# The opening of an encoder layer: x loaded in two halves with the first w_ada group between, and a tile pair of four column pairs by plain blocks

## The chip, the cores and the metric

One core of one Trainium2 chip runs the whole layer in one launch. The metric is the device time of one execution in microseconds (us). TensorE (PE) does the matmuls, VectorE (DVE) and ScalarE (ACT) the element-wise work, GpSimd (POOL) a few small things, and SyncE (SP) issues nearly all DMAs, in the order in which they were written to its queue.

## The reference

Everything is float32. x is (1024, 2048), D = 2048; c is one vector. Cut to what matters here:

```python
mod = silu(c) @ w_ada + b_ada                 # w_ada: (2048, 6144)
shift, scale, gate = split(mod, 3)
h = rmsnorm(x, pre_g) * (1 + scale) + shift   # (1024, 2048)
q, k, v, gate_a, u, gate_p = split(h @ w_in)  # w_in: (2048, 4608)
y_a = windowed_gqa(q, k, v, rel_table, sink) * silu(gate_a)
y_p = multiscale_pool(u, w_pool_grp, pool_scale) * silu(gate_p)
g_a, g_p = split(sigmoid(h @ w_merge + b_merge))   # w_merge: (2048, 4096)
merged = g_a * (y_a @ w_br_attn) + g_p * (y_p @ w_br_pool)
out = x + gate * rmsnorm(merged @ w_out, post_g)
```

The change concerns the way into `h @ w_in`: how x, w_ada and the first columns of w_in come in, and in which order the first products are made.

## The kernel before, in words

**Precision and Strassen.** A float32 operand is kept as two float32r halves, high and low (`split`: ACT copies the high half, DVE subtracts it to get the low one), and a product takes three matmuls: high by high, high by low, low by high. A product of 256 output columns by 1024 rows of x over a part of D is done as one level of Strassen's scheme (`strassen`): seven products X, V, Z, X, V, Z, Z with the moving operands B11, T3, T2, B21, T4, T1, B22. These are made from the four quarters of a pair of tiles of h transposed (two tiles of 128 columns of D, each in a left half of 512 rows of x, s = 0, and a right half, s = 1). A *pair* is such a block of 256 columns of the combined w_in and w_merge: 34 pairs in all. `js` lists the tile pairs of D that a call covers; the first half of D has tile pairs 0 to 3. A pair with two tile pairs has 7 x 3 x 2 = 42 matmuls of 128x512, with four 84.

**The ramp.** At the start h isn't there yet. It becomes ready one tile pair after the other, so the first RAMP = 5 pairs are done in two parts: first over tile pairs 0 and 1, results put away in `ramp_d`, then over tile pairs 2 and 3, with the first part added. The very first pair takes its tile pairs 0 and 1 by *plain blocks* instead (four blocks of 128x512, six matmuls each per tile pair, no Strassen sums). The other pairs of the first pass (`pass1`) take all four tile pairs at once.

**How h comes about.** `fetch_rows_of_x` loads eight groups of 128 rows, four tiles of 512 columns each (256 KB a load). `norm_rows` squares and sums them (two tiles on ACT, two on DVE), takes root and reciprocal, and makes `turn`: a diagonal matrix of 1/rms. `turn_rows` and `turn_round` multiply x's tiles by it on TensorE, which transposes and scales in one go (two matmul records each). `modulation(j)` makes scale and shift for tile pair j: a GEMV over 16 tiles of w_ada (four steps q of eight records), a copy to SBUF (`acc`), four transposes into PM, and DVE's sums into `modc`. `fill(j)` modulates tile pair j and makes all seven moving operands, each high and low; `fill_blocks` and `fill_sums` are the same work in two halves, for the plain blocks and for Strassen.

**Order.** The program is traced and then laid out by a scheduler that goes by priority in program order and by free buffers; instructions handed to `keep` stay in the written order on their engine. The opening is written out by hand in this way. In the ramp, `side` holds steps that are taken one at each of the seven places of a pair (the groups of w_ada for tile pairs 2 and 3, `late_sums`); in the first pass `side` holds the sums of w_ada for the second half of D, taken at the places in `EASY`.

**Buffers that matter.** 56 tiles of 2 KB a partition (`big`) for x, w_ada's groups, xT and the moving operands; four for raw weights; nine `ev` tiles for results on their way out; PSUM tags `mm`, `sc`, `at` with two banks each and `z0`, `z1` (SEEDED) with one.

Of the kernel before, what the change touches and what calls it, by code (L numbers as in the profile page):

```python
# [13 lines left out]
F32 = mybir.dt.float32  # L14
# [29 lines left out]
def encoder_layer(ctx: ExitStack, tc: tile.TileContext, x, c, table, w_ada, b_ada, pre_g,  # L44
# [89 lines left out]
    RAMP = 5  # L134
# [55 lines left out]
    def load_raws(w, n0, rows, js, pin=False):  # L190

        raws = []
        nj = len(js)
        joint = wp.tile([P, 2, nj, 256], F32, tag="raw", name=uid("raw"), bufs=4) if nj < 4 else None
        for kh in range(2):
            r = joint[:, kh] if nj < 4 else wp.tile([P, nj, 256], F32, tag="raw", name=uid("raw"), bufs=4)
# [216 lines left out]
    def norm_rows(si):  # L413
        ssq = ep.tile([P, 8], F32, tag="ssq", name=f"ssq{si}", bufs=4)
        for q in range(4):
            xt = xts[si, q]
            if q < 2:
                junk = bank("sc", "junk")
                ins = nc.scalar.activation(junk, xt, AF.Square, accum_out=ssq[:, q:q + 1])
                if si < 2:  # L420
                    keep(ins)
            else:
                junk = bank("at", "junk")
                nc.vector.scalar_tensor_tensor(junk, xt, 1.0, xt, op0=ALU.mult, op1=ALU.mult,
                                               accum_out=ssq[:, q:q + 1])
        nc.vector.tensor_reduce(ssq[:, 4:5], ssq[:, 0:4], op=ALU.add, axis=AX.X)
        if si == 0:
            small_vectors()
        ins = nc.scalar.activation(ssq[:, 5:6], ssq[:, 4:5], AF.Sqrt, bias=eps_t, scale=1.0 / D)
        if si < 2:  # L430
            keep(ins)
        nc.vector.reciprocal(rstd[:, si:si + 1], ssq[:, 5:6])
# [3 lines left out]
        nc.vector.tensor_scalar(turn[si], ident, rstd[:, si:si + 1], None, op0=ALU.mult)  # L436

    def turn_round(s, q, js):

        banks = [bank(t, "XT1") for t in SEEDED]  # L440

        def turn_one(m, n):
            keep(nc.tensor.matmul(banks[n][:, m * P:(m + 1) * P], xts[4 * s + m, q][:, js[n] * P:(js[n] + 1) * P],
                                  turn[4 * s + m], start=True, stop=True))

        def put_by(both=False):
            if both:
                keep(nc.scalar.activation(xT[q * 4 + js[0], s], banks[0], AF.Copy))
            else:
                keep(nc.vector.tensor_copy(xT[q * 4 + js[0], s], banks[0]))  # L450
            keep(nc.scalar.activation(xT[q * 4 + js[1], s], banks[1], AF.Copy))

        return deque(partial(turn_one, m, n) for m in range(4) for n in range(2)), put_by

    def turn_rows(s):

        for q in range(1):
            banks = [bank(t, "XT1") for t in ("mm", "mm", *SEEDED)]
            for m in range(4):
                for j in range(4):  # L460
                    nc.tensor.matmul(banks[j][:, m * P:(m + 1) * P], xts[4 * s + m, q][:, j * P:(j + 1) * P],
                                     turn[4 * s + m], start=True, stop=True)
            for j in range(4):
                if j % 2 == 0:
                    nc.vector.tensor_copy(xT[q * 4 + j, s], banks[j])
                else:
                    nc.scalar.activation(xT[q * 4 + j, s], banks[j], AF.Copy)
# [132 lines left out]
    def fill_blocks(j, between=None):  # L600

        (b11, b12), (b21, b22) = ((xT[k, 0], xT[k, 1]) for k in (2 * j, 2 * j + 1))
        right = tuple(bp.tile([P, 512], F32R, tag=t, name=uid(t)) for t in ("B12h", "B12l"))
        for n, ((hi, lo), t, k) in enumerate(((op["B11"][j], b11, 2 * j), (op["B21"][j], b21, 2 * j + 1),
                                              (right, b12, 2 * j), (op["B22"][j], b22, 2 * j + 1))):
            keep(modulate(nc.scalar, t, k, hi))
            keep(modulate(nc.vector, t, k))
            if n < 3 or between:
                anchor["blocks"] = sub(lo, t, f32(hi))
                keep(anchor["blocks"])  # L610
            if between:
                between(n)
        return right

    def fill_sums(j, done=False):
# [6 lines left out]
        if not done:  # L622
            hi, lo = op["B22"][j]
            keep(sub(lo, b22, f32(hi)))
# [6 lines left out]
    def ramp_gen(jj, i, parts, **kw):  # L631
        w, n0 = weight_of(ORDER[i])
        dst = block(part_d, ORDER[i]) if jj else block(ramp_d[i], 0)
        return strassen(w, n0, rows_in_turn(0), (2 * jj, 2 * jj + 1), op, ev, to_dram(dst), parts, raws[i], **kw)

    fetch_rows_of_x(0)
    fetch_rows_of_x(1)
    raws = []

    def fetch_raws(i):  # L640
        raws.append(load_raws(*weight_of(ORDER[i]), rows_in_turn(0), [0, 1], True))

    def fetch_half(j):
        w, n0 = weight_of(ORDER[0])
        for kh in range(2):
            keep(load(raws[0][kh][:, j], rows_in_turn(0)(w, [0, 1], kh)[:, j, n0:n0 + 256]))

    ada = [ada_slots(0)]
    joint = wp.tile([P, 2, 2, 256], F32, tag="raw", name=uid("raw"), bufs=4)
    raws.append([joint[:, 0], joint[:, 1]])  # L650
    fetch_half(0)
    ada.append(ada_slots(1))
    fetch_half(1)
    fetch_raws(1)
    fetch_raws(2)
    claim(0)
    ada.append(ada_slots(2))
    claim(1)
    fetch_raws(3)
    ada3 = [ada_tile(3, q) for q in range(5)]  # L660
    ada3 = [at[:, kk] for at in ada3 for kk in range(2)] + ada_slots(3, range(10, KT))
    for i in range(4, RAMP):
        fetch_raws(i)
# [3 lines left out]
    late_sums = {0: group2[:1], 4: group2[1:4], 5: group2[4:], 10: group3[:4], 12: group3[4:]}  # L667
    side = deque((lambda n=n: [step() for step in late_sums.get(n, ())]) for n in range(13))
    for s in range(2):
        for si in range(4 * s, 4 * s + 4):  # L670
            norm_rows(si)
        if s == 0:
            bias_rows()
        turn_rows(s)
    keep(nc.vector.tensor_scalar(nsink_t, sink_t, -1.0, None, op0=ALU.mult))
    weights0 = []

    def first_weights(j):
        hi, lo = (wp.tile([P, 2, 256], F32R, tag=t, name=uid(t), bufs=4) for t in ("whi", "wlo"))
        for kh in range(2):  # L680
            split(hi[:, kh], lo[:, kh], raws[0][kh][:, j], True)
        weights0.append((hi, lo))

    opened, right_top = {}, []

    def plain_block(blk, j):

        nt, s = int(blk[0]) - 1, int(blk[1]) - 1

        def piece(n):  # L690
            if j == n == 0:
                opened[blk] = bank("mm" if s == 0 else "sc", "PB")
            whi, wlo = (w[:, :, nt * P:(nt + 1) * P] for w in weights0[j])
            mov = (op["B11"][j], op["B21"][j]) if s == 0 else (right_top[j], op["B22"][j])
            kh, w, m = ((0, whi, 0), (0, wlo, 0), (1, whi, 0), (1, wlo, 0), (0, whi, 1), (1, whi, 1))[n]
# [991 lines left out]
```

## Time and profile before

| what | value |
|---|---|
| median of 3 runs | 2103.34 us (2102.85 to 2106.11) |
| profiled execution: its span, first to last instruction | 2099.7 us; its own time is told by this span alone, 3.6 us under the median of the runs |
| TensorE busy | 2073.3 us, 99% |
| DVE, ACT busy | 1540.1 us (73%), 1108.6 us (53%) |
| mean granted TensorE clock | 0.998 |
| moved by DMA | 468.20 MB, 223 GB/s over the span |
| first 46.4 us: TensorE busy | 29.22 us, DMA share 0.97 |

How to read the rows that follow. A row of the timeline has the start in us, the duration, engine, source line, operation, what it writes <- what it reads, shape and count, and in brackets how long the engine had been idle before it and what ended that. "PEld" are weight loads, which run beside the matmuls. A busy TensorE isn't TensorE at its peak: ends of matmuls are modelled, so rates are read from starts. A DMA row on SPq is the time of issue; the list of DMA issues gives the median time from there to landing.

### The profile page before, as it was taken

The page shows a single profiled execution, that of the slowest core. Times are in us where ns is not written, and L with a number is a line of the kernel's source. Part 1 is how long each engine was busy: PE and PEld are TensorE (multiplying, and loading weights), DVE is VectorE, ACT ScalarE, POOL GpSimd, SP SyncE. Part 2 cuts the span into 40 slices and gives each one's busy share as a digit, 9 for nine tenths or more (in the row PEclk, how much of TensorE's full clock was granted, in tenths as well). Part 3 has the DMA queues.
Part 4 walks back from the last instruction along what each step waited for, and adds up shares of the span by engine and source line. Part 5 has one row for each costly group of instructions (what it writes and reads, how often), then busy time and mean ns, then how long its engine had stood idle before and what let it go on. Part 6 is the DMA issues. An engine that isn't in the chain of part 4 may idle for free.

```text
span 2099.7 us, 28891 instructions
## 1 busy us (share of the span) xinstructions
PE 2073.3 (99%) x9511; PEld 1709.1 (81%) x9511; DVE 1540.1 (73%) x2769; ACT 1108.6 (53%) x2105; POOL 33.9 (2%) x119
## 2 busy tenths in 40 slices
PE   6999999999999999999999999999999999999998
PEld 4688888888888888888888888888888888888886
DVE  5886777777556766677777678857857977889667
ACT  4754444444574635665665444333645644767654
POOL 0000000000000000000000000010000000000000
PEclk9999999999999999999999999999999999999999
DMA  9888788887675455454554476675745566686997
GB/s 328 292 273 270 226 270 284 273 280 243 214 241 193 136 187 189 158 174 159 186 164 155 160 246 214 217 243 178 251 159 175 168 201 197 225 308 206 292 339 246
DMA packets 302251, 468.20 MB, mean 223 GB/s; under 512 B 23939, under 2 KB 144875, under 8 KB 302100
## 3 DMA queue, kind: packets, MB, share of 16 engines
q1 hardware_dynamic: 297024, 453.60, 66.0%
q0 software_dynamic: 3616, 10.53, 1.3%
q10 hardware_dynamic: 1460, 2.22, 0.3%
q8 instruction: 74, 1.21, 0.2%
q14 instruction: 77, 0.63, 0.1%
HBM read 341.45 MB, written 126.90 MB: 223 GB/s over the span
## 4 chain that ended last, share of the span: by engine, by line
PE 94%; DVE 1%; DMA 1%; ACT 0%; issue 0%; DVEq 0%; SPq 0%; ACTq 0%
PE Z L247 32%; PE X L247 21%; PE V L247 21%; PE Z L1394 2%; PE Z L1396 2%; PE Z L1395 2%; PE X L1396 1%; PE V L1396 1%; PE V L1394 1%; PE X L1394 1%; PE X L1395 1%; PE V L1395 1%; PE PT L1104 1%; PE PV L1115 0%; PE PV L1116 0%; PE PV L1114 0%
## 5 line engine op out<-in xcount | busy, mean ns | idle before, releaser
L96 ACT ACTIVATE whi<-raw 128x512 fp32r<-128x512 f32 (+1 forms) x532 | 321.7, 606 | 517.9 <-PE Z L247 250.9
L97 DVE TENSOR_TENSOR wlo<-raw,whi 128x512 fp32r<-128x512 f32 (+1 forms) x532 | 347.4, 658 | 168.1 <-PE Z L247 133.1
L97 DVE TENSOR_TENSOR wlo<-wr,whi 128x512 fp32r<-128x512 f32 x224 | 150.6, 689 | 50.7 <-ACT whi L96 43.4
L96 ACT ACTIVATE whi<-wr 128x512 fp32r<-128x512 f32 x224 | 138.5, 629 | 86.6 <-DVE wlo L97 29.4
L114 DVE TENSOR_TENSOR raw<-raw,raw 128x512 f32<-128x512 f32 x79 | 54.6, 691 | 85.1 <-DMA raw<-in_w_merge_dram 61.9
L96 ACT ACTIVATE whi<-ws 128x512 fp32r<-128x512 f32 (+1 forms) x88 | 53.7, 610 | 71.6 <-PE X L247 63.8
L247 PE MATMUL Z<-T1h,whi 128*128 128x512 f32 x334 | 91.0, 390 | 0.0
L247 PE MATMUL Z<-B22h,whi 128*128 128x512 f32 x334 | 90.9, 392 | 0.0
L247 PE MATMUL X<-B21h,whi 128*128 128x512 f32 x334 | 90.9, 391 | 0.0
L247 PE MATMUL X<-B11h,whi 128*128 128x512 f32 x334 | 90.7, 390 | 0.0
L247 PE MATMUL V<-T3h,whi 128*128 128x512 f32 x334 | 90.7, 391 | 0.0
L247 PE MATMUL V<-T4h,whi 128*128 128x512 f32 x334 | 90.5, 391 | 0.0
L247 PE MATMUL Z<-T2h,wlo 128*128 128x512 f32 x334 | 90.2, 390 | 0.2 <-DVE wlo L97 0.2
L247 PE MATMUL X<-B11l,whi 128*128 128x512 f32 x334 | 90.4, 390 | 0.0
L247 PE MATMUL Z<-T2h,whi 128*128 128x512 f32 x334 | 90.2, 390 | 0.2 <-ACT whi L96 0.2
L247 PE MATMUL Z<-T1l,whi 128*128 128x512 f32 x334 | 90.3, 389 | 0.0
L247 PE MATMUL Z<-B22l,whi 128*128 128x512 f32 x334 | 90.2, 390 | 0.0
L247 PE MATMUL X<-B21l,whi 128*128 128x512 f32 x334 | 90.2, 390 | 0.0
L247 PE MATMUL V<-T3l,whi 128*128 128x512 f32 x334 | 90.2, 390 | 0.0
L247 PE MATMUL V<-T4l,whi 128*128 128x512 f32 x334 | 90.2, 389 | 0.0
L247 PE MATMUL Z<-T1h,wlo 128*128 128x512 f32 x334 | 90.1, 389 | 0.0
L247 PE MATMUL V<-T3h,wlo 128*128 128x512 f32 x334 | 90.1, 389 | 0.0
(364 smaller groups left out, 4822.0 us busy)
## 6 DMA issues: line engine op xcount, KB each, us to landing
part<-part_d SPq DMA_DIRECT2D x136, 256.0 KB, 4.7
ada<-in_w_ada_dram SPq DMA_DIRECT2D x128, 256.0 KB, 5.8
raw<-in_w_merge_dram SPq DMA_DIRECT2D x64, 512.0 KB, 5.4
raw<-in_w_in_dram SPq DMA_DIRECT2D x62, 512.0 KB, 4.0
wr<-ws_dS SPq DMA_DIRECT2D x60, 512.0 KB, 5.3
wr<-in_w_out_dram SPq DMA_DIRECT2D x48, 512.0 KB, 5.2
proj_d<-part SPq DMA_DIRECT2D x68, 256.0 KB, 2.2
sw<-in_w_out_dram SPq DMA_DIRECT2D x64, 256.0 KB, 5.5
```

Source lines behind the costliest of these rows:

```text
L96: ins = (nc.scalar.activation(hi, src, AF.Copy), nc.vector.tensor_tensor(lo, src, f32(hi), ALU.subtract))
L97: nc.vector.tensor_tensor(lo, src, f32(hi), ALU.subtract))
L114: return (eng or nc.vector).tensor_tensor(o, a, b, ALU.add)
L247: nc.tensor.matmul(ps, w_[:, i], op[mov][j][m_], start=fresh and i == 0 and n == 0, stop=i == nj - 1 and n == 2, skip_group_check=True)
L1104: nc.tensor.transpose(pt[:, i * P:(i + 1) * P], p[:, i * P:(i + 1) * P], ident)
L1394: nc.tensor.matmul(pb, hi, w[0], start=first, stop=False, skip_group_check=True)
L1395: nc.tensor.matmul(pb, lo, w[0], start=False, stop=False, skip_group_check=True)
L1396: nc.tensor.matmul(pb, hi, w[1], start=False, stop=last, skip_group_check=True)
```

## The change

- The loads' order on SP: rows 0 to 511 of x, w_ada's first group, 512 columns of w_in for tile pair 0 (`wide`, four loads), then rows 512 to 1023, w_ada's second group, and the weights of the next pairs.
- Four pairs (K, V, and the first two of gate_a) take tile pair 0 by plain blocks, 16 blocks of six matmuls; their second part then covers tile pairs 1, 2 and 3. Four more pairs take tile pairs 0 and 1 by Strassen and then 2 and 3. RAMP is 8.
- The left half (s = 0) of all eight tiles of x's first half of columns is turned at once. Then the eight left blocks are written in turn with `norm_rows` 4 to 7 (all kept now, with the squares written over x's own tiles of columns 1024 to 2047), with `turn_first` (the first two tiles of the right half) and with `scale_rows`, which scales the other six tiles on ACT so that `turn_later` can turn them by a plain transpose.
- `fill_half` replaces `fill_blocks`. Tile pair 1 has no plain blocks: its GEMV comes between the last right blocks, and `fill(1)` is unpinned ahead of the ramp.
- The groups of w_ada for tile pairs 2 and 3 are summed at steps 13 to 25 of the ramp, not 0 to 12. The first pass has 17 pairs in its first stretch, not 20, with up to five side steps a pair.

```diff
-    RAMP = 5
+    AHEAD_PAIRS = 4
+    RAMP = 8
...
-        joint = wp.tile([P, 2, nj, 256], F32, tag="raw", name=uid("raw"), bufs=4) if nj < 4 else None
+        joint = wp.tile([P, 2, nj, 256], F32, tag="raw", name=uid("raw"), bufs=4) if nj < 3 else None
...
     def norm_rows(si):
-        for q in range(4):
-            xt = xts[si, q]
-            if q < 2:
-                junk = bank("sc", "junk")
...
+        for q in (2, 3, 0, 1):
+            xt, junk = xts[si, q], xts[si, q | 2]
+            if q % 2 == 0:
+                keep(nc.scalar.activation(junk, xt, AF.Square, accum_out=ssq[:, q:q + 1]))
             else:
+                keep(nc.vector.scalar_tensor_tensor(junk, xt, 1.0, xt, op0=ALU.mult, op1=ALU.mult,
+                                                    accum_out=ssq[:, q:q + 1]))
...
     def turn_rows(s):
-        for q in range(1):
+        for q in range(2):
...
+    def turn_first(m):
+        for k in range(2):
+            if m == 0:
+                late_banks[k] = bank(SEEDED[k], "XT1")
+            keep(nc.tensor.matmul(late_banks[k][:, m * P:(m + 1) * P], xts[4 + m, 0][:, k * P:(k + 1) * P],
+                                  turn[4 + m], start=True, stop=True))
+
+    def scale_rows(si):
+        for q, c0 in ((0, 2 * P), (1, 0)):
+            part = xts[si, q][:, c0:512]
+            keep(nc.scalar.activation(part, part, AF.Copy, scale=rstd[:, si:si + 1]))
+
+    def turn_later(k, n):
+        pt = bank(SEEDED[n % 2], "XT2")
+        for m in range(4):
+            keep(nc.tensor.transpose(pt[:, m * P:(m + 1) * P], xts[4 + m, k // 4][:, k % 4 * P:(k % 4 + 1) * P], ident))
+        if n % 2:
+            keep(nc.vector.tensor_copy(xT[k, 1], pt))
+        else:
+            keep(nc.scalar.activation(xT[k, 1], pt, AF.Copy))
...
+    def fill_half(s):
+        names = ("B11", "B21") if s == 0 else ("B12", "B22")
+        for k, name in enumerate(names):
+            src = xT[k, 0] if s == 0 else late_banks[k]
...
+            keep(modulate(nc.scalar, src, k, hi))
+            keep(nc.vector.tensor_scalar(xT[k, s], src, modc[:, 1, k, 0:1], modc[:, 0, k, 0:1],
+                                         op0=ALU.mult, op1=ALU.add))
+            keep(sub(lo, xT[k, s], f32(hi)))
...
     fetch_rows_of_x(0)
+    ada = [ada_slots(0)]
+    fetch_wide(0)
+    fetch_wide(1)
+    claim(0)
     fetch_rows_of_x(1)
     ada.append(ada_slots(1))
+    ramp_raws(4, (0, 1))
+    ramp_raws(5, (0, 1))
+    claim(1)
     ada.append(ada_slots(2))
+    ramp_raws(6, (0, 1))
     ada3 = [ada_tile(3, q) for q in range(5)]
...
+    ramp_raws(7, (0, 1))
...
-    late_sums = {0: group2[:1], 4: group2[1:4], 5: group2[4:], 10: group3[:4], 12: group3[4:]}
+    late_sums = {13: group2[:1], 16: group2[1:4], 17: group2[4:], 23: group3[:4], 25: group3[4:]}
...
+    def plain_block(i, nt, s):
+        ps = bank(("mm", "sc")[blocks[0] % 2], "PB")
+        whi, wlo = (w[:, :, nt * P:(nt + 1) * P] for w in weights0[i])
+        mov = (op["B11"][0], op["B21"][0]) if s == 0 else (right["B12"], op["B22"][0])
+        for n, (kh, w, m) in enumerate(((0, whi, 0), (0, wlo, 0), (1, whi, 0), (1, wlo, 0), (0, whi, 1), (1, whi, 1))):
+            keep(nc.tensor.matmul(ps, w[:, kh], mov[kh][m], start=n == 0, stop=n == 5, skip_group_check=True))
+        t = ev.tile([P, 512], F32, tag="ev", name=uid("c"))
+        if blocks[0] % 2:
+            keep(nc.vector.tensor_copy(t, ps))
+        else:
+            keep(nc.scalar.activation(t, ps, AF.Copy))
+        store(block(ramp_d[i], 0)(f"{nt + 1}{s + 1}"), t)
+        blocks[0] += 1
+
+    g0 = modulation(0, ada[0].__getitem__, True)
+    for step in g0[:4]:
+        step()
+    wide_weights(0)
+    fill_half(0)
+    wide_weights(1)
+    norm_rows(4)
+    plain_block(0, 0, 0)
+    plain_block(0, 1, 0)
+    turn_first(0)
+    scale_rows(4)
+    wide_weights(2)
+    plain_block(1, 0, 0)
+    norm_rows(5)
+    plain_block(1, 1, 0)
+    turn_first(1)
+    scale_rows(5)
...
+    plain_block(3, 0, 0)
+    norm_rows(7)
+    plain_block(3, 1, 0)
+    turn_first(3)
+    fill_half(1)
+    scale_rows(7)
...
+    plain_block(0, 0, 1)
+    turn_next(1)
+    plain_block(0, 1, 1)
+    turn_next(1)
+    fill_sums(0)
+    plain_block(1, 0, 1)
+    turn_next(2)
+    plain_block(1, 1, 1)
+    turn_next(2)
+    s0, s1, s2, s3, _ = modulation(1, ada[1].__getitem__, True)
+    plain_block(2, 0, 1)
     s0()
+    plain_block(2, 1, 1)
     s1()
+    plain_block(3, 0, 1)
     s2()
+    s3()
+    plain_block(3, 1, 1)
...
     held.close()
+    fill(1)
...
-    EASY = ((0, 2, 4, 6), (1, 3, 5))
-    n1 = 20
+    EASY = ((0, 2, 4, 6), (0, 1, 3, 5, 6), (0, 2, 4, 6))
+    n1 = PAIRS - RAMP - 9
```

More of the change, by code (lines that the diff above doesn't have):

```diff
@@ L435, in norm_rows @@
         turn[si] = turn["all"][:, (si % 4) * P:(si % 4 + 1) * P]
[L436 to L453, printed above, removed]
+        keep(nc.vector.tensor_scalar(turn[si], ident, rstd[:, si:si + 1], None, op0=ALU.mult))
     def turn_rows(s):
-        for q in range(1):
+        for q in range(2):
             banks = [bank(t, "XT1") for t in ("mm", "mm", *SEEDED)]
@@ L636, in encoder_layer @@
     fetch_rows_of_x(0)
+    ada = [ada_slots(0)]
+    fetch_wide(0)
+    fetch_wide(1)
+    claim(0)
     fetch_rows_of_x(1)
[L638 to L649, printed above, removed]
@@ L684, in encoder_layer @@
[L684 to L695, printed above, removed]
-            keep(nc.tensor.matmul(opened[blk], w[:, kh], mov[kh][m], start=j == n == 0,
-                                  stop=j == 1 and n == 5, skip_group_check=True))
-            if j == 1 and n == 5:
-                t = ev.tile([P, 512], F32, tag="ev", name=uid("c"))
-                keep(nc.scalar.activation(t, opened[blk], AF.Copy))
-                store(block(ramp_d[0], 0)(blk), t)
-        return [partial(piece, n) for n in range(6)]
```

175 lines of the change are left out of this document (59 added, 116 removed).

## The prediction

> **What bounds the kernel now.** I read the page first (busy shares, the chain that ended last), then busy time by stage, then the first 113 us instruction by instruction.
>
> ```profile
> span 2099.7 us, 28891 instructions
> PE 2073.3 (99%) x9511; PEld 1709.1 (81%) x9511; DVE 1540.1 (73%) x2769; ACT 1108.6 (53%) x2105; POOL 33.9 (2%) x119
> PE 94%; DVE 1%; DMA 1%; ACT 0%; issue 0%; DVEq 0%; SPq 0%; ACTq 0%
> 0.00:46.40 46.40, 29.22 (x151) 20.51 (x152) 21.20 (x71) 22.64 (x58) 3.02 (x34) 0.93 0.97 326
> 46.40:69.50 23.10, 22.53 (x117) 13.05 (x117) 20.69 (x42) 14.01 (x26) 1.24 (x14) 1.00 1.09 346
> 69.50:112.50 43.00, 43.00 (x224) 31.32 (x221) 38.53 (x88) 32.89 (x73) 0.00 (x0) 1.00 0.83 270
> 160.00:540.00 380.00, 380.00 (x1685) 312.63 (x1684) 271.59 (x402) 159.65 (x260) 6.73 (x13) 1.00 0.80 263
> 183.68 5.44 PE Z L247 x24
> ```
>
> (Stage rows: length, then busy time and count of PE, weight loads, DVE, ACT, POOL, then granted clock, DMA share, GB/s.) TensorE works without a gap from 69.5 us on and carries 94% of the chain; 24 of its 128x512 matmuls take 5.44 us, 0.227 each. So only two things can move the time: how many matmuls are left when TensorE becomes dense, and any new gap behind that point. Ahead of 46.4 us it waits for loads; from 46.4 to 69.5 it stood still 0.6 us in all. The reference point is the first V product behind the opening:
>
> ```profile
> 69.48 0.73 PE L247 MATMUL V<-T3h,whi 128*128 128x512 f32 x2
> ```
>
> **The change, by parts.** The loads are the first part.
>
> ```profile
> 0.74 11.40 SPq L411 DMA_DIRECT2D xt<-in_x_dram  x15
> 11.71 8.03 SPq L411 DMA_DIRECT2D xt<-in_x_dram  x12
> 24.09 5.87 SPq L497 DMA_DIRECT2D ada<-in_w_ada_dram  x9
> xt<-in_x_dram SPq DMA_DIRECT2D x48, 256.0 KB, 5.4
> ada<-in_w_ada_dram SPq DMA_DIRECT2D x128, 256.0 KB, 5.8
> 42.19 0.14 PEld L512 LDWEIGHTS GEMV<-ada,scz 128*32 128x32 f32 x2 [0.61 <-DMA ada<-in_w_ada_dram]
> ```
>
> The fifteenth load of x has been issued by 12.1 us; the sixteenth follows and lands 5.4 later, near 18. A load of x takes 0.67 us of the queue (12 in 8.03), one of w_ada 0.75 (256 KB at 346 GB/s). With 16 loads of x ahead of w_ada's first group, not 32, that group has landed at 18 + 16 x 0.75 = 30, not 42.2; the four `wide` loads at 33; rows 4 to 7 of x at 35.7, 38.4, 41.1 and 43.7; w_ada's second group at 55.7.
>
> From the last landing to the first plain block I take the rows of before, 12.2 us earlier:
>
> ```profile
> 43.27 0.60 ACT L519 ACTIVATE acc<-GEMV 128x512 f32<-128x512 f32 x1 [1.75 <-PE GEMV L512]
> 45.53 0.81 ACT L567 ACTIVATE B11h<-xT,modc 128x512 fp32r<-128x512 f32 x1 [1.06 <-issue]
> 46.40 0.50 PE L696 MATMUL PB<-B11h,whi 128*128 128x512 f32 x1 [0.71 <-ACT B11h L567]
> 48.28 0.69 DVE L117 TENSOR_TENSOR B21l<-xT,B21h 128x512 fp32r<-128x512 f32 x1
> 49.02 0.50 PE L696 MATMUL PB<-B21l,whi 128*128 128x512 f32 x1
> ```
>
> So acc at 31.1, first block at 34.2, its last half (B21l) at 36.8. This is the gain: plain blocks start 12.2 us sooner.
>
> What follows loses it. Eight blocks of the left half stand in one written order with rows 4 to 7, and every instruction of that order is kept. On ACT the copy of a block (`plain_block` i,0,0) stands ahead of the next row's squares (`norm_rows`). The rows of one such round:
>
> ```profile
> 13.22 0.58 ACT L419 ACTIVATE junk<-xt 128x512 f32<-128x512 f32 x1
> 13.83 0.58 ACT L419 ACTIVATE junk<-xt 128x512 f32<-128x512 f32 x1
> 27.71 0.16 DVE L426 TENSOR_REDUCE ssq<-ssq 128x1 f32<-128x4 f32 x1
> 28.42 0.29 DVE L436 TENSOR_SCALAR turn<-ident,rstd 128x128 f32<-128x128 f32 x1
> 28.76 0.38 PE L461 MATMUL XT<-turn,xt 128*128 128x128 f32 x1 [0.41 <-DVE turn L436]
> 64.59 1.09 ACT L700 ACTIVATE c<-PB 128x512 f32<-128x512 f32 x2
> 35.86 2.05 PE L443 MATMUL XT<-turn,xt 128*128 128x128 f32 x16
> ```
>
> Two tiles turned (4 records of 0.12 each): 0.5. A block, 6 x 0.227: 1.4, and 0.2 to its end. Its copy 0.55. Two squares at 0.61, with their read 1.4. Reduce to the next turning (27.71 to 28.76) 1.05. Together 5.1 us a row, of which TensorE has 3.3 us of work: 1.8 us lost in each round. The first turning comes at 40.05 (DVE: 36.8, two weight splits to 37.4, two squares to 39.0, then 1.05); the others at 45.2, 50.3, 55.4. The right half's first block then starts at 56.8 (B12h 0.8 us) and ends at 59.2 with its low half. Rows have landed by 43.7, so loads don't set this.
>
> Next, two blocks, two turned tiles, and `fill_sums(0)`:
>
> ```profile
> 51.13 0.68 DVE L117 TENSOR_TENSOR xT<-xT,xT 128x512 f32<-128x512 f32 x1
> 57.16 0.69 DVE L97 TENSOR_TENSOR T1l<-xT,T1h 128x512 fp32r<-128x512 f32 x1
> 55.46 1.06 PE L512 MATMUL GEMV<-ada,scz 128*32 128x512 f32 x8
> 43.94 0.64 PE L480 MATMUL PM<-ident,acc 128*128 128x128 f32 x4
> ```
>
> Those sums took 6.7 us, 6.1 without the B22l that moves. They start at 62.7 (behind two DVE copies) and end at 68.8. The copies that free banks z0 and z1 for the fifth and sixth turned tile stand behind them on ACT and DVE, so TensorE stands still from 65.4 to 69.2 and has its last tile at 70.3. Then four blocks (1.36 each) and four steps of GEMV (1.05 each, 8 records) with the last block behind them: GEMV done at 78.5, though its data landed at 55.7. `modc` is ready 2.3 later (43.27 to 45.53) at 80.8. `fill(1)` must make T3 low before V's fourth matmul: two scalings, three sums in a chain (51.13 and its like), five more of 0.6 each on DVE, 6.3 us, so 87.1. V then counts as started at 86.4.
>
> Matmuls: four pairs by 24 plain and 63 Strassen (7 x 3 x 3), 87 against 84; before, one pair by 48 + 42. That is +6. At V after, 48 more plain ones are behind it: 42 fewer left, -9.5 us; and 8 GEMV records more, +1.1. The 24 turned tiles in one record each (0.16 in PM's row, against 0.26 in XT's) lie ahead of V. Opening: 86.4 - 69.5 - 9.5 + 1.1 = **+8.5 us**.
>
> Later group sums: the third GEMV's columns come at step 25 of 28, so `fill(3)` has two Strassen products before the second half begins.
>
> ```profile
> 91.79 0.60 PE L480 MATMUL PM<-ident,acc 128*128 128x128 f32 x4
> 94.54 0.16 DVE L490 SCALAR_TENSOR_TENSOR modc<-modc,cols 128x2 f32<-128x2 f32 x1
> 104.20 0.69 DVE L97 TENSOR_TENSOR T3l<-xT,T3h 128x512 fp32r<-128x512 f32 x1
> 112.70 0.61 PE L247 MATMUL X<-B11h,whi 128*128 128x512 f32 x2
> ```
>
> Here T3l came 13.1 us after PM on a DVE that was full (38.53 of 43.0), and nobody waited. After, V of the second half wants it 0.6 + 2 x 1.36 + 9 x 0.227 + 5 x 0.227 = 6.5 us after PM. Upper bound 13.1 - 6.5 = 6.6; lower, on an idle DVE (43.94 to 45.53 is 1.6, then 6.3, less 6.5), 1.4. I take **+4.0**, between them, since pairs 6 and 7 leave DVE some room.
>
> Queues. SP takes the loads in the new order without a stop up to w_ada's second group: of the 56 `big` buffers 12 hold xT, 16 x's first half, 16 w_ada's first group, and the later ones come free by 31 us. The third group does wait: 12 + 14 + 14 + 16 buffers are full until the second GEMV runs, so it is issued from about 72 on and lands by 72 + 16 x 0.75 + 5.8, near 91; step 13 asks for it at 86.4 + 12 x 1.36 = 103. POOL's 14 marks of `claim(1)` wait for x's second half (70.3) and are wanted at 80.8. Both cost nothing; if step 13 came at 86, the same wait would be 5 us.
>
> At nothing too: `scale_rows` (8 ACT copies, 4 us; ACT waits for blocks meanwhile; in the open at most 1 us for the last row); squares written to SBUF (0.1 us a square either way); three more pairs in two parts (6 MB more, at the 0.83 and 0.80 DMA share of the stages above there is room; cover gone, 6 MB at 346 GB/s is 18 us of queue, some 3 us of wait); 4.3 side steps a pair, not 3.5, in the first pass (DVE busy 72%, TensorE 19 us a pair). Ends 0 and +3 for the last two.
>
> Sum: 2103.3 + 8.5 + 4.0 = 2116 us, made against the span of 2099.7, which lies 3.6 under the median of the runs shown.
>
> A word on the clock.
>
> ```profile
> 21.30:24.70 3.40, 0.65 (x7) 0.49 (x5) 3.19 (x10) 3.02 (x9) 0.00 (x0) 1.00 1.06 395
> 24.70:28.10 3.40, 3.40 (x16) 3.40 (x16) 2.63 (x10) 2.01 (x9) 0.00 (x0) 0.50 1.05 382
> ```
>
> A stretch of 3.4 us with TensorE busy for 0.65 was followed by one at half clock. The gap of 3.8 us at 65.4 could do the same: 3.4 us at half, +1.7, so 2118. I leave it out, since stretches that straddle the gap are busy in part. The Trainium skill (TensorE: Matmul & The Clock Gate, HAM oscillation — how this bites in real kernels) asks for no idle gap over about 3.4 us; by that rule the sum would be 2118, and these two rows agree with it.
>
> **Rivals.**
> Faster: TensorE stays dense from the first plain block, as it did from 46.4 to 69.5. Work from 34.2 to V: 104 matmuls 23.6, turned tiles 5.8, GEMV 4.2: 67.8; from the last GEMV step to T3 low are 8.6 us, and one block, X and half of V cover 3.9 of them: 72.5. Opening 72.5 - 69.5 - 9.5 + 1.1 = -5.4; with the low 1.4 for `fill(3)`: 2099. It needs each row's scale ready while blocks run, a round of 3.3 us. Against it: two ACT squares and the copy are kept in order.
> No change: the squares overlap the block ahead of them (three rounds, -5.4), `fill_sums(0)` doesn't queue behind the two DVE copies (-1.4), and `fill(3)` costs its low end: 2103.3 + 8.5 - 6.8 + 1.4 = 2106. The remaining gap behind `fill_sums` and the late GEMV eat the earlier start. For it speaks that DVE and ACT have idle time in every round; against it, as above, the written order.
> Slower still: the copies' buffers.
>
> ```profile
> 80.27 2.58 SPq L701 DMA_DIRECT2D ramp_d<-c  x4
> ramp_d<-c SPq DMA_DIRECT2D x12, 256.0 KB, 5.2
> 86.04 0.60 ACT L320 ACTIVATE c<-Z 128x512 f32<-128x512 f32 x1 [1.68 <-DMA ramp_d<-c]
> ```
>
> Copies ready at 66 were stored at 80.3, behind loads, and ACT waited for a buffer. After, 16 copies go through the same nine; the tenth is wanted at 61.5. If 14 loads (two pairs' weights and ten of w_ada's, 10.5 us) stand ahead of the first store on SP, which is through with w_ada's second group and two pairs at 53, that store lands at 53 + 10.5 + 5.2 = 69: +7.5, 2123. It decides as soon as the first store is issued after 56. Against it: the first three copies are ready by 43, ahead of those loads.
>
> **How the numbers follow.** The forecast (2109 to 2122 alone) 0.56, buffers 0.14, no change 0.13, faster 0.17. Faster or slower means by over 0.2%, 4.2 us, about what a measurement tells apart: slower 0.70, same 0.13, faster 0.17. The range 2098 to 2125 reaches from the faster rival to the buffers with 2 us.
>
> **What would show it.** First plain block near 34; turnings of x's second half about 5 us apart with TensorE idle between; a gap of about 4 us behind `fill_sums(0)`; the second GEMV near 72 to 78; V near 86; a wait for T3l when the second half begins. Wrong if the rounds are near 3.3 us, if row loads land after 50, or if TensorE is dense before 75.

## The result, and the profile after

The changed kernel takes 2132.8 us (median, 2130.3 to 2135.6), the kernel before 2103.6: a ratio of 1.0139 (95% interval 1.0124 to 1.0153), 29.2 us slower. The forecast was +12.7 (2116, range 2098 to 2125): right in sign, too small by 16.5 us.

The page, then busy time by stage (length, busy time and count of PE, weight loads, DVE, ACT and POOL, granted clock, DMA share, GB/s):

```profile
span 2133.8 us, 28930 instructions
PE 2079.5 (97%) x9493; PEld 1709.6 (80%) x9493; DVE 1554.5 (73%) x2790; ACT 1111.6 (52%) x2111; POOL 33.3 (2%) x119
PE 92%; DMA 4%; DVE 3%; ACT 1%; issue 0%; SPq 0%; DVEq 0%; POOL 0%; ACTq 0%; POOLq 0%
```

```profile
0.00:35.89 35.89, 18.81 (x104) 13.11 (x104) 12.43 (x41) 15.72 (x36) 2.33 (x34) 0.90 0.94 307
35.89:59.80 23.91, 17.49 (x65) 12.35 (x65) 14.73 (x43) 15.36 (x39) 0.59 (x6) 0.86 1.06 353
59.80:93.90 34.10, 24.97 (x120) 15.20 (x120) 20.65 (x39) 14.87 (x28) 0.79 (x8) 0.95 0.66 223
93.90:139.60 45.70, 44.27 (x226) 30.67 (x224) 30.88 (x70) 29.66 (x60) 0.00 (x0) 1.00 0.62 211
139.60:163.20 23.60, 15.40 (x56) 12.45 (x57) 18.10 (x34) 10.45 (x20) 0.00 (x0) 0.78 0.67 215
```

Before, TensorE was dense from 46.4 us on but for 0.6 us. Here it stands still for 6.4 us in the left half (second row), for 9.1 in the right half and the fill (third), and for 8.2 once more at 140 us (fifth), a place that had no gap before. The chain of work tells the same: TensorE's share fell from 94% to 92%, DMA's rose from 1% to 4%.

To see where the 29 us come in, I compared the times at which equal numbers of Strassen matmuls are left in both traces: +17.0 at 139 us, just ahead of the last stand, +28.3 at 163 us, about +31 at 410, +34 at the end. (Between 94 and 139 us the count doesn't compare, since the two kernels sum w_ada's later groups at different places.) Of the 17.0, 1.4 are a wait at 108.6 us, so some 15.6 belong to the opening. The profiled execution is 2.8 us above its median and that of the kernel before some 2 us below its own, so the traces show about 5 us more than the medians. What TensorE waited for from 34 to 165 us (total, times, longest):

```profile
PE X L248 <- ACT whi L96: 8.2, 1, 8.2
PE XT L467 <- ACT xT L471: 5.4, 1, 5.4
PE XT L454 <- DVE turn L431: 5.2, 3, 1.7
PE PB L697 <- ACT B11h L571: 1.6, 1, 1.6
```

The timeline at the two largest waits (in brackets the idle time of the engine and what ended it):

```profile
55.80 21.15 SPq L703 DMA_DIRECT2D ramp_d<-c  x12
65.26 0.42 ACT L96 ACTIVATE whi<-raw 128x256 fp32r<-128x256 f32 x1 [0.75 <-PE PB L697]
65.70 0.42 DVE L97 TENSOR_TENSOR wlo<-raw,whi 128x256 fp32r<-128x256 f32 x1 [2.54 <-ACT whi L96]
68.04 0.68 DVE L117 TENSOR_TENSOR xT<-xT,xT 128x512 f32<-128x512 f32 x1
70.28 0.42 ACT L96 ACTIVATE whi<-ws 128x256 fp32r<-128x256 f32 x1 [4.60 <-PE PB L697]
74.72 0.68 DVE L97 TENSOR_TENSOR T1l<-xT,T1h 128x512 fp32r<-128x512 f32 x1
75.62 1.97 PE L467 MATMUL XT<-ident,xt 128*128 128x128 f32 x8 [5.38 <-ACT xT L471]
88.34 0.16 DVE L494 SCALAR_TENSOR_TENSOR modc<-modc,cols 128x2 f32<-128x2 f32 x1
...
141.34 1.57 SPq L198 DMA_DIRECT2D raw<-in_w_in_dram  x3
147.22 0.52 ACT L96 ACTIVATE whi<-raw 128x384 fp32r<-128x384 f32 x1 [2.09 <-DMA raw<-in_w_in_dram]
147.80 1.65 PE L248 MATMUL X<-B11h,whi 128*128 128x512 f32 x3 [8.21 <-ACT whi L96]
```

`fill_sums(0)` ran from 68.04 to 75.4 (forecast: 62.7 to 68.8). Among and ahead of its kept instructions stand weight splits of the fifth ramp pair (`whi`, `wlo`, `ws`), which are not kept and were put there by the scheduler. They wait for buffers that plain blocks still read. The second half's first weights went out at 141.34, right behind the last pair's stores on SP.

### The profile page after: what moved, and what is told of

The parts are those of the page before. It is cut to its first block, busy times and chain, and to the rows that moved or that the text cites. A ratio compares the mean times of both kernels' runs of the same rounds, so it can differ in the third digit from the quotient of the medians.

```text
span 2133.8 us, 28930 instructions
## 1 busy us (share of the span) xinstructions
PE 2079.5 (97%) x9493; PEld 1709.6 (80%) x9493; DVE 1554.5 (73%) x2790; ACT 1111.6 (52%) x2111; POOL 33.3 (2%) x119
## 4 chain that ended last, share of the span: by engine, by line
PE 92%; DMA 4%; DVE 3%; ACT 1%; issue 0%; SPq 0%; DVEq 0%; POOL 0%; ACTq 0%; POOLq 0%
PE Z L248 30%; PE X L248 20%; PE V L248 20%; PE Z L1388 2%; PE Z L1390 2%; PE Z L1389 2%; PE X L1389 1%; PE X L1390 1%; PE X L1388 1%; PE V L1389 1%; PE V L1388 1%; PE V L1390 1%; PE PT L1098 1%; DMA ada<-in_w_ada_dram 1%; PE PB L697 1%; DMA xt<-in_x_dram 1%
## 5 line engine op out<-in xcount | busy, mean ns | idle before, releaser
L96 ACT ACTIVATE whi<-raw 128x512 fp32r<-128x512 f32 (+2 forms) x528 | 319.3, 606 | 529.7 <-PE Z L248 261.3
L97 DVE TENSOR_TENSOR wlo<-raw,whi 128x512 fp32r<-128x512 f32 (+2 forms) x528 | 344.2, 655 | 172.1 <-PE Z L248 133.2
L114 DVE TENSOR_TENSOR raw<-raw,raw 128x512 f32<-128x512 f32 (+1 forms) x80 | 54.6, 683 | 75.8 <-DMA raw<-in_w_merge_dram 56.7
L96 ACT ACTIVATE whi<-ws 128x512 fp32r<-128x512 f32 (+2 forms) x88 | 53.4, 607 | 77.2 <-PE X L248 66.4
L114 DVE TENSOR_TENSOR u<-V,u 128x512 f32<-128x512 f32 x94 | 64.6, 687 | 38.6 <-PE V L248 37.6
L248 PE MATMUL X<-B11h,wlo 128*128 128x512 f32 x332 | 90.3, 392 | 0.0
```

Of the source, the lines that this page charges most:

```text
L96: ins = (nc.scalar.activation(hi, src, AF.Copy), nc.vector.tensor_tensor(lo, src, f32(hi), ALU.subtract))
L97: nc.vector.tensor_tensor(lo, src, f32(hi), ALU.subtract))
L114: return (eng or nc.vector).tensor_tensor(o, a, b, ALU.add)
L248: nc.tensor.matmul(ps, w_[:, i], op[mov][j][m_], start=fresh and i == 0 and n == 0, stop=i == nj - 1 and n == 2, skip_group_check=True)
```

## The experiments

All times below are set against the kernel before as run with them, so "+22.5" is us above that. In brackets stand the ratio and its 95% interval, which leaves each figure some 2.5 to 3 us either way.

**1. The second half's weights earlier.**

```diff
+        gen = ramp_gen((0, 1), i, None, False)
+        if i == RAMP - 1:
+            ramp_raws(0, (1, 2, 3))
+        run(gen, ...)
...
-    for i in range(RAMP):
+    for i in range(1, RAMP):
         ramp_raws(i, ...)
```

> The two weight loads of the ramp's second half, first pair, are traced ahead of the eighth ramp pair's work instead of behind its last store; nothing else moves. In the changed kernel TensorE stood still from 139.6 to 147.8 there, the first split ended its wait on such a load (147.22), and the granted clock was half from 143.3 to 153.5. Theory A (these loads, issued at 141.34 behind the stores, made the gap): the gap shrinks from 8.2 to 0 to 2 us and the half clock goes too, 8 to 11 us off the changed kernel's 2132.8: 2122 to 2125. Rival B (fill(3) sets the end, as the prediction had it, with +4.0): T3 low comes at 143.9 to 144.5 whatever the loads do, V waits some 2 to 4 us for it instead, the gain is 3 to 5 us: 2128 to 2130.

Measured: 2126.4, +22.5 (ratio 1.0108, 1.0093 to 1.0123), 6.7 less than the change. The load's issue, and the stage that was 23.6 us with the stand in it:

```profile
127.45 1.01 SPq L198 DMA_DIRECT2D raw<-in_w_in_dram  x2
```

```profile
139.20:163.20 24.00, 23.27 (x102) 18.78 (x102) 20.17 (x38) 13.70 (x28) 0.00 (x0) 1.00 0.67 217
```

TensorE lost 0.7 us there instead of 8.2, at full clock. T3 low of tile pair 3 came at 144.5, as theory B said, but nobody waited for it. Theory A holds for the mechanism; 2126.4 lies in neither range (A's 8 to 11 us and B's 3 to 5).

**2. The fifth pair's splits pinned behind the last plain block.**

```diff
     plain_block(3, 1, 1)
+    split(*first[0], a11, True)
+    keep(sub(s3, a11, a21))
+    split(*first[1], s3, True)
...
-        run(ramp_gen((0, 1), i, None, False), ...
+        run(ramp_gen((0, 1), i, None, False, first if i == AHEAD_PAIRS else ()), ...
```

> The two weight splits of the fifth ramp pair and the difference between them are made in a written order, behind the last plain block, instead of at a place of the scheduler's choosing among the plain blocks. In the changed kernel they stood on ACT and DVE ahead of the right half's copies and of fill_sums, and waited for weight buffers that plain blocks held (ACT 0.75 and 4.60 us, DVE 2.54). Theory A (those waits push fill_sums from 62.7-68.8 to 68.0-75.4 and make the 5.4 us stand of TensorE before 75.6 with the half clock after it): fill_sums ends near 69 to 70, the stand shrinks to 0 to 3 us, V starts near 88 and not 93.9, 4 to 7 us off: 2126 to 2129. Rival B (the two DVE copies and the two ACT copies between the tiles set fill_sums, and the splits only fill time that is lost anyway): under 1.5 us off, 2131 to 2133.

Measured: 2138.5, +34.5 (1.0166, 1.0151 to 1.0182), 5 us worse. DVE's first and last instruction of `fill_sums`, and TensorE's waits:

```profile
65.27 0.68 DVE L117 TENSOR_TENSOR xT<-xT,xT 128x512 f32<-128x512 f32 x1
71.30 0.68 DVE L97 TENSOR_TENSOR T1l<-xT,T1h 128x512 fp32r<-128x512 f32 x1
```

```profile
PE XT L467 <- ACT xT L471: 4.1, 1, 4.1
PE V L248 <- ACT T3h L96: 2.3, 1, 2.3
PE Z L248 <- ACT whi L96: 2.1, 1, 2.1
```

Without the splits among it `fill_sums` takes 6.7 us and the stand is 4.1; the prediction had 6.1 and 3.8, the changed kernel 7.4 and 5.4. So the splits explain most of the longer stand and about half of the longer sums. But a stand is left without them, and the splits, now among `fill(1)`, made V and Z wait for 4.4 us. Both theories missed the time.

**3. The squares a block earlier.**

```diff
     plain_block(0, 0, 0)
+    norm_rows(5)
     plain_block(0, 1, 0)
...
     plain_block(1, 0, 0)
-    norm_rows(5)
+    norm_rows(6)
     plain_block(1, 1, 0)
...                      # and so on for rows 6 and 7
```

> The squares and the scale of rows 5, 6 and 7 of x stand one plain block earlier in the written order: right behind the copy of the first block of the round before, so each row is ready while the round before it runs. Theory A (the prediction's round: the block's copy and then the next row's two squares in one order on ACT cost 1.8 us of TensorE in each round): turnings 3.3 to 4 us apart instead of 5.2, the right half's first block at 54.5 to 56.5 instead of 59.8, and all behind it as much earlier: 3 to 5 us off the changed kernel, 2128 to 2130. Rival B (the right half is late for another reason: the GEMV, fill(1) and the fifth pair's splits set V, with slack in front of them): the right half starts earlier but V still starts within 1.5 us of 93.9: 2131 to 2133.

Measured: 2130.8, +26.9 (1.0131, 1.0114 to 1.0148). The right half's first block starts at 52.56, and no wait for `turn` is left:

```profile
40.42 0.68 PE L454 MATMUL XT<-turn,xt 128*128 128x128 f32 x4 [0.54 <-PE PB L697]
43.69 0.60 PE L454 MATMUL XT<-turn,xt 128*128 128x128 f32 x4
46.88 0.71 PE L454 MATMUL XT<-turn,xt 128*128 128x128 f32 x4
```

Rounds of 3.2 us, the last 4.0 (theory A). Yet the median fell by 2 us only, which with these intervals is not told from none; its runs spread from 2127.3 to 2132.3, and the profiled one is the shortest. Experiment 12 asks again for the worth of the edit.

**4. The second GEMV ahead of the right half.**

```diff
+    for step in modulation(1, ada[1].__getitem__, True)[:4]:
+        step()
     plain_block(0, 0, 1)
...
-    s0()                 # and s1 to s3 among the last four blocks
```

> The four steps of the second w_ada group's GEMV stand ahead of the right half's first plain block instead of among its last four blocks; its loads have landed by then. Theory A (the opening ends with a chain GEMV, modc, fill(1), V that starts at 79.35 and ends at 94.3, and its place in the written order is what makes V late): V starts 5 to 8 us earlier, 2125 to 2128. Rival B (ACT and DVE are late through fill_sums and the copies, so fill(1) can't start before them): the acc copy queues behind and V starts at most 2 us earlier, and may start later by what 4.2 us of GEMV ahead of fill_sums push: 2131 to 2136.

Measured: 2133.2, +29.2 (1.014, 1.0125 to 1.0155): nothing. `modc` was ready at 62.9 and not 88.3, but the loads of w_ada's third group now went out at 59.93, ahead of the first store (68.25), and a copy waited for a buffer:

```profile
68.25 5.77 SPq L703 DMA_DIRECT2D ramp_d<-c  x8
73.69 0.69 DVE L700 COPY c<-PB 128x512 f32<-128x512 f32 x1 [4.80 <-DMA ramp_d<-c]
75.03 1.11 PE L467 MATMUL XT<-ident,xt 128*128 128x128 f32 x4 [7.28 <-DVE xT L469]
```

Theory B has the size, by another mechanism: this is the prediction's rival of the copies' buffers.

**5. The kernel before, with eight ramp pairs alone.** The later pairs' weights are fetched at step 3 of earlier ones.

```diff
-    RAMP = 5
+    RAMP = 8
...
-    EASY = ((0, 2, 4, 6), (1, 3, 5))
-    n1 = 20
+    EASY = ((0, 2, 4, 6), (0, 1, 3, 5, 6), (0, 2, 4, 6))
+    n1 = PAIRS - RAMP - 9
```

> The kernel before with one part of the change alone: eight ramp pairs and not five, the later pairs' weights fetched at step 3 of an earlier pair, and the first pass laid out as in the changed kernel (4.3 side steps a pair). Opening and loads of x stay as they were. Theory A (the prediction's 'at nothing', 0 to +3 for three more pairs in two parts and 0 to +3 for the denser side steps; the changed kernel lost 3.4 us more than before between 163 us and 1640 us of its span, and 1.8 at the end, so these parts do cost): 2105 to 2109. Rival B (that loss in the first pass belongs to something else, such as the order of loads that the opening leaves behind): 2102 to 2105, within 1.5 of the kernel before.

Measured: 2107.2, +4.1 (1.003, 1.0019 to 1.0042): theory A. At equal matmuls left it is level with before (within 0.6 us) until 200 us, then loses 1.3 near 258, 2.5 near 375 and 0.9 between 1640 and 1865 us. Two waits of the first pass:

```profile
258.07 1.21 PE L247 MATMUL V<-T3h,whi 128*128 128x512 f32 x4 [1.26 <-ACT whi L96]
375.31 1.04 PE L885 MATMUL PMR<-acc,onez 128*32 128x512 f32 x2 [1.26 <-DVE acc L536]
```

**6. `fill_sums(0)` behind the last turned tiles.**

```diff
-    fill_sums(0)
     plain_block(1, 0, 1)
     turn_next(2)
     plain_block(1, 1, 1)
     turn_next(2)
+    fill_sums(0)
```

> fill_sums(0) of the changed kernel stands behind the last turned tiles of x's second half instead of behind the second one. Theory A (the stand of TensorE from 70.2 to 75.6 is the copies that free banks z0 and z1, queued behind fill_sums' kept splits and sums on ACT and DVE; the pinned weight splits left it at 4.1): the stand goes, the last tile turns near 70 to 72 and not 77.2, and V starts 4 to 7 us earlier: 2126 to 2129. Rival B (the sums have to be done before V in any case, and fill(1) stands behind them on DVE: the stand only moves): V within 1.5 us of 93.9, now with TensorE waiting for T3 or T2, 2131 to 2134.

Measured: 2132.3, +29.1 (1.014, 1.0127 to 1.0153). The stand of 5.4 us is gone and X starts at 84.35, 6.3 earlier (1.3 of that this execution had ahead of the right half already): theory A for the mechanism. But the two stands behind it stayed or grew, two new stretches came at half clock, and the time did not move:

```profile
PE X L248 <- ACT whi L96: 8.3, 1, 8.3
PE Z L248 <- ACT u L258: 2.3, 1, 2.3
```

```profile
87.08:90.50 3.42, 3.42 (x9) 2.66 (x10) 2.85 (x6) 1.88 (x5) 0.00 (x0) 0.50 1.11 350
107.56:110.97 3.41, 3.41 (x13) 1.22 (x12) 1.12 (x2) 0.91 (x2) 0.00 (x0) 0.50 0.87 332
```

From X to the stand near 140 us this trace takes 53.0 us, the changed kernel's 49.0: 0.9 more of stands and 3.1 more of busy time, about what 6.8 us at half clock lose.

**7. Edits 1, 3 and 6 together.**

> Three edits of the changed kernel together: the second half's first weights fetched ahead of the eighth ramp pair, the squares of rows 5 to 7 a block earlier, fill_sums(0) behind the turned tiles. Theory A (three separate places in one order of time, so the gains add: 6.4 us by the first alone, 2 to 6 by the second, 4 to 6 by the third): 2115 to 2121. Rival B (each gain ahead of V ends at the same later wait, fill(1) on DVE and ACT, so that only the first and one of the others show): 2122 to 2127.

Measured: 2120.5, +17.4 (1.0078, 1.0066 to 1.009): theory A. One large stand is left, behind copies' buffers: the last four stores stood behind 16 loads of w_ada's fourth group.

```profile
92.55 4.12 SPq L703 DMA_DIRECT2D ramp_d<-c  x4
99.69 0.60 ACT L258 ACTIVATE u<-Z 128x512 f32<-128x512 f32 x1 [4.16 <-DMA ramp_d<-c]
100.34 1.22 PE L248 MATMUL Z<-T1h,whi 128*128 128x512 f32 x2 [4.81 <-ACT u L258]
```

**8. As 7, the second GEMV among the right half's first blocks.**

```diff
+    s0()
+    s1()
     plain_block(1, 0, 1)
...
+    s2()
+    s3()
     plain_block(1, 1, 1)
     turn_next(2)
     fill_sums(0)
+    fill(1)
```

> The three edits together, and the four GEMV steps of the second w_ada group stand among the right half's first four blocks (two by two) with fill(1) traced behind fill_sums(0). Theory A (TensorE has about 20 us of work from the right half's first block to V, and DVE some 20 us as well, so V can start near 78 to 82 from a right half at 52.6): 4 to 8 us below the three edits alone, 2108 to 2115. Rival B (as when the GEMV alone was put earlier, the copies and sums on ACT and DVE are pushed as far as the GEMV gains): within 2 us of the three edits alone.

Measured: 2122.6, +19.5 (1.0091, 1.0078 to 1.0104). That is 2.1 us above experiment 7, at the edge of theory B, but again by the buffers: the first store went out late, and DVE stood still.

```profile
62.84 6.29 SPq L703 DMA_DIRECT2D ramp_d<-c  x9
68.21 0.69 DVE L700 COPY c<-PB 128x512 f32<-128x512 f32 x1 [7.96 <-DMA ramp_d<-c]
```

**9. As 7, with the last four stores ahead.**

```diff
-    ada3 = [ada_tile(3, q) for q in range(5)]      # ahead of the plain blocks
-    ramp_raws(7, (0, 1))
...
     plain_block(3, 1, 1)
+    at3 = [ada_tile(3, q) for q in range(5)]
+    ada3.extend(...)
+    ramp_raws(7, (0, 1))
```

> The three edits together (2120.5), with the loads of w_ada's fourth group and of the eighth pair's weights traced behind the last plain block, so that the last four stores of plain blocks go out ahead of them on SP. Theory A (the copies' buffers: with V started 13 us earlier, TensorE stood still from 95.54 to 100.34 because ACT's u waited 4.16 us for a buffer whose store was issued at 92.55 behind 16 loads of w_ada; half clock from 97.9 to 104.7 came of it): the stand goes, 4 to 8 us off, 2112 to 2117. Rival B (the loads that are pushed back are late instead: the third and fourth group's GEMV wait, or the second half's weights): the stand moves to 100-135, 2118 to 2123.

Measured: 2111.7, +8.4 (1.004, 1.0028 to 1.0053), 9 us less than experiment 7: theory A, slightly beyond its range. The stores went out at 79.01, and TensorE has no stand of 0.7 us or more from 80.3 to 163 us:

```profile
79.01 2.57 SPq L701 DMA_DIRECT2D ramp_d<-c  x4
```

```profile
79.01:163.20 84.19, 82.81 (x393) 62.01 (x392) 65.72 (x133) 50.85 (x102) 0.00 (x0) 1.00 0.73 241
```

Not all of the 9 us need be the stores: experiment 7's runs fall into two groups (2117 and 2120.5 to 2120.9), and its profiled one, of the slower, has in the first pass a wait of 1.95 us at 385 us and 3.4 us at half clock behind it, which experiment 9's trace doesn't have. Experiment 9 is the best version of the change that I found, and still slower than the kernel before.

**10. As 9, the GEMV right behind `fill_sums(0)`.**

```diff
     fill_sums(0)
+    for step in modulation(1, ada[1].__getitem__, True)[:4]:
+        step()
     plain_block(2, 0, 1)
-    s0()                 # and s1 to s3 among the last four blocks
```

> As the run with the stores ahead, and the four GEMV steps of the second w_ada group right behind fill_sums(0) and ahead of the last four plain blocks, not among them. Theory A (what is left of the opening is the chain GEMV, modc, fill(1) behind the last block; DVE is free from 72 to 75): V 2 to 4 us earlier than 81, 2110 to 2115 in all and 2 to 4 below the run with the stores ahead. Rival B (fill_sums and fill(1) keep DVE and ACT busy in a chain, so modc just waits): within 1.5 us of that run.

Measured: 2112.9, +9.6 (1.0046, 1.0034 to 1.0059): theory B. The GEMV's copy queues behind the sums' splits on ACT, which experiment 9's order hides behind the last blocks:

```profile
71.84 0.58 ACT L523 ACTIVATE acc<-GEMV 128x512 f32<-128x512 f32 x1
```

```profile
72.47 1.11 PE L484 MATMUL PM<-ident,acc 128*128 128x128 f32 x4 [4.00 <-ACT acc L523]
```

**11. As 10, seven ramp pairs, 18 pairs of four side steps.**

```diff
-    RAMP = 8
+    RAMP = 7
...
-    late_sums = {13: group2[:1], 16: group2[1:4], 17: group2[4:], 23: group3[:4], 25: group3[4:]}
+    late_sums = {9: group2[:1], 11: group2[1:4], 12: group2[4:], 16: group3[:4], 18: group3[4:]}
...
-    EASY = ((0, 2, 4, 6), (0, 1, 3, 5, 6), (0, 2, 4, 6))
+    EASY = ((0, 2, 4, 6),)
```

> As the run with the GEMV behind the sums, with seven ramp pairs and not eight, hence 18 pairs of the first pass with four side steps each (72 in all) instead of 17 with 4.3; the group sums at steps 9 to 18 instead of 13 to 25. Theory A (of the 4.1 us that eight pairs cost the kernel before by themselves, the denser side steps make most: there 1.26 us of V waiting for a weight split and 1.26 us of the row sums waiting): 1.5 to 3.5 us below. Rival B (the group sums have too little room with three ramp pairs: the fourth group's data lands near 96 and fill(3) follows late, so TensorE stands still before the second half): 3 us or more above.

Measured: 2116.1, +12.9 (1.0062, 1.0049 to 1.0076), 3.3 us above experiment 10. Theory B has the size by the medians, though the two profiled executions differ by 0.7 us only, and not the place: there is no stand before the second half. The first pass still waits, now at two places:

```profile
247.63 1.21 PE L248 MATMUL Z<-B22h,whi 128*128 128x512 f32 x4 [1.21 <-ACT whi L96]
266.75 1.20 PE L248 MATMUL V<-T3h,whi 128*128 128x512 f32 x4 [2.47 <-DVE u L114]
```

From 163 to 410 us it loses 4.5 us against the kernel before, experiment 10 loses 4.4. So the number of side steps a pair alone isn't the cause of experiment 5's 4.1 us; what is stays open.

**12. As 9, without edit 3.** The diff of experiment 3 taken back.

> The run with the stores ahead (2111.65) with the squares of rows 5 to 7 put back to the changed kernel's place; the other three edits stay. In the kernel with nothing else repaired, the squares moved the right half's first block from 58-60 to 52.6 and V by 6 us in the trace, but the times told only 2 +- 3 us. Theory A (the rounds do cost what the trace shows, and the second half's stand and the copies' buffers hid part of it there): 4 to 7 us slower than 2111.65, so 2115.5 to 2118.5, with turnings 5.2 us apart. Rival B (the rounds' idle time is made good later, since ACT and DVE set V): within 2 us, 2110 to 2114.

Measured: 2117.5, +13.4 (1.0065, 1.0052 to 1.0079). Theory A: the rounds cost 5.0 us (13.4 - 8.4) where no large stand follows; no run of experiment 9 is as slow as the fastest here (2114.1 against 2114.7). Why experiment 3's median showed less stays open; the stand at 140 us and the copies' buffers were still in it (6.5 and 1.1 us).

**The account.** Differences between kernels, each above before: late weights 29.2 - 22.5 = 6.7; the place of `fill_sums` and the order of the stores together 22.5 - 13.4 = 9.1; rounds 13.4 - 8.4 = 5.0; eight pairs 4.1; what is left of the opening 8.4 - 4.1 = 4.3. Sum 29.2, as it must be: the last term is what is left. Each term carries the intervals of two ratios, so 5.0 is told from nothing and not from 3 or 7; the 4.1 was measured in the kernel before. The split depends on the order of the edits: alone, edit 6 was worth nothing.

## Why the prediction was wrong

Three terms of the sum failed. In the traces, the opening was +8.5 and came to about +15.6: right path, sizes too small. The second half's start was +4.0 for a late T3 low, and came to +11.3 (28.3 - 17.0) by another wait, for weights, and the half clock it brought. The terms "at nothing" were 0, and came to +4.1 in experiment 5. The clock, left out, has a part in the first two.

**The round: right.** Forecast 5.1 us a row, 1.8 of it lost; measured 5.18 and 5.19 between the last three turnings, with 1.7 us of wait in each, and 5.0 us for the rounds in all. The start was later than forecast (first block 35.89, not 34.2; first turning 41.69, not 40.05), but that lies in this execution: in the other eleven traces with this opening they come at 34.2 to 35.4 and 40.0 to 41.2. The first round took 6.4, part of it at half clock (0.86 over that stage).

**The opening: mechanism right, +8.5 mis-sized; measured about +15.6.** The right half began 3.0 us late (59.80, not 56.8), by the late start and the first round. Three more pieces are missing from the walk. The right half's low halves were ready about 1 us later than reckoned from the first block on; DVE's read of the PSUM tile waited 0.79 us for ACT's. `fill_sums(0)` began 5.3 us late in all, 8.2 behind the right half's first block; in experiment 2, without the splits, it was 6.7. So some 1.5 us of this are the unpinned splits of the next pair, which wait for weight buffers of the plain blocks; I had walked only kept instructions in the written order. And the stand behind it was 5.4, not 3.8, with half clock after it. Its place and cause (the copies that free z0 and z1) were as forecast: experiment 6 removed it.

**`fill(3)` late, +4.0: fell.** It cost nothing: with the weights early (experiment 1), X starts the second half within 0.7 us while T3 low arrives at 144.5. The forecast had TensorE take X and then V; in that trace it takes parts of Z between them (from 142.20 us on) and doesn't stand. The second half did begin with a stand, of twice the size (8.2 us), for a DMA. I asked of SP's queue whether loads came in time up to w_ada's third group, and not when the second half's weights are issued. In the kernel before they are traced without `keep` and went out at 94.46 and 104.39; in the change `ramp_raws` pins them, and they went out behind the last pair's stores. Experiment 1 moved their place in the order; the pin by itself was not tried.

**The clock: left out.** The stand at 140 us lasted 8.2 us, and what came behind it ran at half clock:

```profile
143.30:146.71 3.41, 0.00 (x0) 0.00 (x0) 1.95 (x4) 1.26 (x3) 0.00 (x0) 0.50 0.97 281
146.71:153.53 6.82, 5.73 (x14) 4.48 (x15) 5.35 (x11) 3.21 (x7) 0.00 (x0) 0.50 0.46 148
```

The second row alone is 6.8 us at half clock, 3 us of work lost (half of 5.73); experiment 1's trace has neither. The stand before 75.6 was followed by 3.4 us at half clock as well. And all twelve traces with this opening have half clock for 3.4 or 6.8 us near the first plain blocks, from 34.8 to 37.5 us on, behind waits of 0.8 and 1.6 us at most; the walk has nothing of it. The Trainium skill's rule that the prediction set aside (TensorE: Matmul & The Clock Gate, HAM oscillation — how this bites in real kernels) agrees with both stands: 5.4 and 8.2 us, above its 3.4, were followed by half clock. The two rows that the prediction showed for it don't bear it out: the longest stand in them is 2.75 us (before 24.68 us), under 3.4.

**"At nothing": 4.1 us.** Three more pairs and denser side steps had been given 0 to +3 each and were taken as 0. Experiment 5 gives their sum, all of it behind 200 us, so in the first pass and not in the ramp.

**The rivals.** The copies' buffers: with the first store at 62.84 or 68.25 (experiments 8 and 4) the wait came, 8.0 and 4.8 us long. In the changed kernel the first store went out at 55.80, just ahead of my 56, and the opening saw no such wait; a small one came at 109 us, behind the last four stores (ACT 0.75 us, TensorE 1.4). The threshold itself isn't shown: nothing was tried between 55.80 and 62.84, and in experiment 7 two copies waited 1.0 and 2.9 us with the first store at 55.00. I priced this as one case among others; it met the repairs of the opening in experiments 4, 7 and 8, until experiment 9 moved the stores. The faster rival needed rounds of 3.3 us; experiment 9 has two of 3.2 and is still 8.4 us above before. It had reckoned with full clock and without the eight pairs: in that trace 10.2 us run at half clock between 34.8 and 58.8 us, some 5 us of work lost, and the eight pairs cost 4.1. Its chain from the last GEMV step to T3 low was right: 8.6 us, measured 8.5.

## What to carry to other kernels

Where only part of an order is pinned, walk the unpinned instructions too: what the scheduler puts ahead of a kept instruction can wait for a buffer (ACT's split 4.60 us here), and everything kept waits behind it. For each new stage of work ask when its loads are issued, and which stores and loads stand ahead of them on the queue; here the loads issued from 141.34 on let the first split start at 147.22, and TensorE stood still for 8.2 us. What a repair gains at its place can be lost again behind it: edit 6 alone had X 6.3 us earlier and the end nowhere, through half clock and a longer wait for a copy's buffer. Edit 3 was worth 2 us alone and 5.0 with the others.

## What the runs showed of the hardware

Half clock came in stretches of 3.4, 6.8 or 10.2 us in the opening, and often without a long stand. In experiment 9, a stretch with TensorE busy for 1.98 of 3.42 us, its longest stand 1.02, was followed by one at half clock:

```profile
51.88:55.30 3.42, 1.98 (x6) 0.86 (x6) 2.92 (x4) 1.87 (x4) 0.00 (x0) 1.00 1.11 349
55.30:58.71 3.41, 3.41 (x10) 2.78 (x11) 0.43 (x1) 1.19 (x2) 0.00 (x0) 0.50 1.09 365
```

In experiment 12 a stretch with still less work was not:

```profile
49.30:52.70 3.40, 1.67 (x10) 1.16 (x9) 2.10 (x8) 2.60 (x7) 0.20 (x2) 1.00 1.10 348
52.70:56.10 3.40, 2.38 (x11) 1.62 (x9) 0.92 (x5) 2.09 (x6) 0.20 (x2) 1.00 1.10 349
```

In each trace the changes of the clock lie whole multiples of 3.41 us apart, which gives windows to count in. Over the 14 traces, from 15 us after the start to 12 us before the end, 8501 such windows have full clock. Of those with TensorE busy for under 46% of the window all 25 are followed by half clock; of those between 46% and 65%, 15 of 65; of the 8411 above, none. So in these traces it goes with the busy share of a window and not with one long stand. What decides between 46% and 65% was not found.
